# Two lone mixers of a diffusion transformer: four delta-net chunks prepared together, then four state steps

## The chip, the cores and the metric

One core of a Trainium2 chip. The metric is the device time of one execution in microseconds.

## What is computed

Two layers of a transformer block over 256 latent tokens (s = 0) and 256 context tokens (s = 1), width 1024. Each layer modulates by columns computed from a condition (`silu(c) @ ada_w`), runs a hybrid mixer (attention beside a gated delta rule in both directions) and then a PEER feed-forward, which fetches 128 experts per token from tables.

```python
mod_lat = (jax.nn.silu(c) @ ada_w[l] + ada_b[l])[:, None, :]
h_lat = rmsnorm(x, norm1_w[l]) * (1.0 + sc1) + sh1
...
A = jnp.where(strict, jnp.einsum('nbhid,nbhjd->nbhij', kb, kc) * decay, 0.0)
Tm = jnp.eye(C, dtype=jnp.float32) + A
u = lax.linalg.triangular_solve(Tm, vc * bc[..., None], ...)
w = lax.linalg.triangular_solve(Tm, kb * jnp.exp(gcum)[..., None], ...)
qk = jnp.einsum('nbhid,nbhjd->nbhij', qc, kc) * decay
def step(S, xs):
    v_new = u_i - jnp.einsum('bhcd,bhde->bhce', w_i, S)
    o_i = (jnp.einsum('bhcd,bhde->bhce', q_i * jnp.exp(g_i)[..., None], S)
           + jnp.einsum('bhij,bhje->bhie', qk_i, v_new))
    S = (S * jnp.exp(g_last)[..., None]
         + jnp.einsum('bhcd,bhce->bhde', k_i * jnp.exp(g_last - g_i)[..., None], v_new))
...
x = x + g1 * o_lat
x = x + g2 * peer_ffn(h2, peer_wq[l], peer_subkeys[l], peer_u[l], peer_v[l])
```

The inverse of `Tm`, `w` and `qk` of a chunk need no state S; only `step` does.

## The kernel before

Of the four mixers two run with nothing beside them: mixer(1, 0) at the start and mixer(0, 1) in the middle. They are called with `big=True` and write each operand of their projections as a high and a low part (`_hi`, `_lo`; `whi`, `wlo` for weights), three matmuls for one. The other two mixers lie under the fetching of experts.

A lone mixer runs in this order. `norm1` (L345) squares and scales the two token tiles (128 tokens each; `xn`), transposes them into the bank `ps_n`, and applies scale and shift on ScalarE (`hf`), from which `hT_hi` and `hT_lo` are made. `dn_gates` makes the gates g and beta from `ps_ba`; `dn_project` makes q, k and v (`ps_dn`), one weight tile of 512 KB for 128 columns. Then `dn_scan` (L733) runs over 2 x 2 chunks: token tiles 0 and 1 forward (d = 0), 1 and 0 backward (d = 1). `dn_chunk` (L605) is the state-free part: gate sums (`ps_g`), decay (`ps_R`, E), `ps_KK`, the mask B, the start of X and its transpose M, `ps_QK`, and six levels that build the inverse; a level is `ps_P` from M and B, its copy Pm on ScalarE, `ps_X` from X and Pm, and VectorE's masked copy into X (`COPY_PREDICATED X<-clev,ps_X`) with M transposed anew. `dn_step` (L698) is the step with the state: `ps_y`, `ps_o`, `ps_S`. Before, the two chunks of a step i go through `dn_chunk` in lockstep, their two `dn_step` follow, and then comes the next pair.

Beside the scan runs a filler, one of its pieces per yield times `rate`: attention's projections (`ps_pr` from `in_rows`), attention itself (`ps_as`, `ps_pT`, `ps_ao`), the gate's projection, and then `modulation` (L279) of chunks 4 to 9. What of the filler is left when the scan ends follows it, and then chunk 10. These seven chunks read 28 weight tiles `ada_t`, for each two matmuls into `ps_ada`, after four of them a copy `row` and four small matmuls into `ps_adat`. These lines decide the order of the filler and of the splits:

```python
for _ in main:            # _with_filler
    due += n
    while due >= 1:
        next(filler, None)
        due -= 1
...
w = (pool or self.wpool).tile([P, D], F32, tag="w", name="w")     # weight, L194
self.nc.sync.dma_start(w, self.ap[name][l, i])
...
hi = self.hlpool.tile([P, D], F32R, tag="whi", name="whi")
lo = self.hlpool.tile([P, D], F32R, tag="wlo", name="wlo")
self.split(w, hi, lo)
```

wpool has four buffers; a weight's load is issued on SyncE's queue once the matmuls of the tile four before it are done. hlpool holds the split parts; the split is a cast on ScalarE (whi) and a subtraction on VectorE (wlo). After the scan `dn_output` norms O (`dO`) and multiplies it by the gate, transposes it (`ps_yT`), and the out projection reads `out_t`.

A scheduler sets the final order of each engine's instructions from the code's order and its own estimate of times, so the order below is read from the built program. All VectorE work is recorded under L131, the line of a helper.

Of the kernel before, what the change touches and what calls it, by code (L numbers as in the profile page):

```python
# [20 lines left out]
P = 128  # L21
# [125 lines left out]
class Net:  # L147
# [196 lines left out]
    def norm1(self, pool, s, pr, hl):  # L344
# [3 lines left out]
        with self.pool(f"n1{s}") as pn:  # L348
            ss = pn.tile([P, 2 * NT], F32, name="n1ss")
            xn = []  # L350
            for t in range(NT):
                for n in range(2):
                    self.square_sum(pn, x, ss, t, n)
# [3 lines left out]
                xn.append(xt)  # L357
            for g in range(KB // 2):
                ps = self.dbank("ps_n1")
                for j in range(2):  # L360
                    for t in range(NT):
                        self.transpose(ps[:, j * T + t * P : j * T + t * P + P], xn[t][:, _blk(2 * g + j, P)])
                for j in range(2):
                    kb = 2 * g + j
                    a, b = pr["acol"][:, s, 0, kb : kb + 1], pr["mod"][:, s, kb : kb + 1]
                    if hl:
                        f = pn.tile([P, T], F32, tag="hf", name="hf", bufs=2)
                        hi, lo = (part[:, kb, :] for part in h)
# [3 lines left out]
                    elif j == 0:  # L372
                        self.dve.tensor_scalar(h[0][:, kb, :], ps[:, _blk(j, T)], a, b, op0=ALU.mult, op1=ALU.add)
                    else:
                        nc.scalar.activation(h[0][:, kb, :], ps[:, _blk(j, T)], AF.Identity, bias=b, scale=a)
# [227 lines left out]
    def dn_chunk(self, pool, dn, t, d, it):  # L603
# [11 lines left out]
        def mk(name):  # L615
            return pool.tile(shape, F32, tag=f"{name}{d}", name=f"{name}{d}")
# [83 lines left out]
    def dn_step(self, pool, it, vtok, d, S, O, first_o, new_S):  # L700
# [7 lines left out]
        y = pool.tile([P, DNH, P], F32, tag=f"Pm{d}", name="y")  # L708
# [24 lines left out]
    def dn_scan(self, pool, dn, s, O):  # L733
# [43 lines left out]
    def mixer(self, s, l, pr, big, filler=(), rate=1, late_mods=(), late_consts=None):  # L777
# [4 lines left out]
        with self.pool("mx" + nm) as pa:  # L782
# [533 lines left out]
```

## Time and profile before

| | us |
|---|---|
| runs of the kernel | 2882.13, 2885.86, 2894.39 (median 2885.86) |
| profiled execution | 2888.39, span 2886.6 |
| first lone mixer: first scan | 111 to 259 |
| second lone mixer: second scan | 1961 to 2126 |

TensorE is busy for 65% of the span, VectorE for 64%, ScalarE for 37%, GpSimd for 32%, and the mean granted clock of TensorE is 0.735 of full speed. These are means over stages of very different kinds: while experts are fetched, the DMA engines are busy at 0.9 and more; in the lone mixers hardly any expert moves, and each engine's own table counts. So the lone mixers have to be read in their own stretches.

### The profile page before, as it was taken

What the parts mean: (1) busy time and instruction counts of PE and PEld (TensorE: products, weight loads), DVE (VectorE), ACT (ScalarE), POOL (GpSimd) and SP (SyncE); (2) the same over time, 40 slices, a digit from 0 to 9 for tenths busy, and PEclk for the clock granted to TensorE, in tenths of its full rate; (3) what the DMA queues carried; (4) which work ended last, traced back from release to release, by engine and by line L of the source; (5) the groups of instructions that cost most, each with busy time, mean ns of one, the idle gap of its engine ahead of it and who ended that gap; (6) DMA issues with size and microseconds to landing.
All of it is one profiled execution on the core that took longest, in us unless ns stands there. A gap on an engine that the chain in (4) does not pass through costs nothing.

```text
span 2886.6 us, 37977 instructions
## 1 busy us (share of the span) xinstructions
PE 1888.9 (65%) x12928; PEld 1089.0 (38%) x12928; DVE 1837.9 (64%) x4902; ACT 1066.9 (37%) x2583; POOL 918.4 (32%) x772
## 2 busy tenths in 40 slices
PE   7998844478768888445876644488989544434444
PEld 5876721044336556111544400077767210000000
DVE  4854598465477768974676644487545986544444
ACT  4532333265354334332644322264233332222222
POOL 0000234433244432443243444200002444435552
PEclk8999965579889999556888855599999655555555
DMA  7334799999989999999999999831258999999997
GB/s 281 106 110 168 261 359 363 419 418 364 333 314 364 390 378 390 378 419 418 382 384 371 418 420 419 343 122 40 106 187 302 419 419 419 419 370 420 419 420 293
DMA packets 163311, 961.60 MB, mean 333 GB/s; under 512 B 20784, under 2 KB 28336, under 8 KB 64816
## 3 DMA queue, kind: packets, MB, share of 16 engines
q0 software_dynamic: 110592, 805.36, 69.2%
q1 hardware_dynamic: 52528, 153.83, 15.3%
q8 instruction: 104, 1.70, 0.2%
q14 instruction: 87, 0.71, 0.1%
HBM read 945.48 MB, written 1.05 MB: 328 GB/s over the span
## 4 chain that ended last, share of the span: by engine, by line
DMA 40%; PE 30%; DVE 18%; ACT 6%; issue 4%; POOL 1%; SPq 0%; POOLq 0%; DVEq 0%; ACTq 0%
DMA G<-in_peer_uv,idx 35%; DVE junk L131 6%; PE ps_pq L899 4%; PE acc L1084 3%; DMA h2r<-h 2%; PE ps_P L675 2%; PE ps_dn L208 2%; PE ps_pr L208 2%; PE ps_X L681 2%; PE ps_ada L298 1%; PE ps_pr L211 1%; PE ps_pr L210 1%; PE ps_pr L212 1%; DVE si L131 1%; DMA w<-in_ada_t 1%
## 5 line engine op out<-in xcount | busy, mean ns | idle before, releaser
L1039 POOL DMA_INDIRECT G<-in_peer_uv,idx x768 | 918.2, 1196 | 1934.3 <-PE acc L1084 743.3
L131 DVE CUSTOM_DVE_ANT_0 junk<-G,h2r 128x1024 bf16<-128x1024 f32 x768 | 937.3, 1220 | 511.0 <-DMA G<-in_peer_uv,idx 496.7
L1084 PE MATMUL acc<-G,dg 128*32 128x256 f32 x6144 | 704.9, 550 | 826.5 <-ACT dg L1080 823.2
L1084 PEld LDWEIGHTS acc<-G,dg 128*32 128x32 f32 x6144 | 148.7, 129 | 1321.2 <-ACT dg L1080 1275.8
L1079 ACT ACTIVATE dg<-cident,act 128x32 f32<-128x32 f32 x768 | 246.6, 321 | 1067.4 <-DVE act L131 1031.4
L1080 ACT ACTIVATE dg<-dg,pgate 128x32 f32<-128x32 f32 x768 | 246.4, 321 | 23.3
L899 PE MATMUL ps_pq<-h2T,w 128*128 128x256 f32 x768 | 181.0, 396 | 0.0
L899 PEld LDWEIGHTS ps_pq<-h2T,w 128*128 128x128 f32 x768 | 151.0, 200 | 28.2 <-issue 7.4
L675 PE MATMUL ps_P<-M,B 128*128 128x128 f32 x768 | 115.5, 299 | 32.4 <-DVE M L131 29.5
L675 PEld LDWEIGHTS ps_P<-M,B 128*128 128x128 f32 x768 | 101.5, 206 | 66.4 <-issue 30.7
L131 DVE COPY_PREDICATED X<-clev,ps_X 128x512 f32<-128x512 int8 x96 | 69.7, 728 | 72.6 <-PE ps_X L681 72.6
L681 PE MATMUL ps_X<-X,Pm 128*128 128x128 f32 x768 | 106.1, 284 | 2.4 <-ACT Pm L677 2.4
L681 PEld LDWEIGHTS ps_X<-X,Pm 128*128 128x128 f32 x768 | 95.9, 196 | 18.2 <-issue 7.5
L131 DVE TENSOR_TENSOR wlo<-w,whi 128x1024 fp32r<-128x1024 f32 (+1 forms) x66 | 78.7, 1194 | 36.7 <-ACT whi L181 36.7
L677 ACT COPY Pm<-ps_P 128x512 f32<-128x512 f32 x96 | 56.0, 584 | 121.4 <-PE ps_P L675 121.2
L181 ACT CAST whi<-w 128x1024 fp32r<-128x1024 f32 (+1 forms) x66 | 67.3, 1023 | 71.6 <-PE ps_pr L212 36.3
L1079 ACT ACT_TABLE_LOAD x60 | 77.0, 1283 | 22.1 <-DVE act L131 21.2
L208 PE MATMUL ps_dn<-hT,w 128*128 128x256 f32 x320 | 84.0, 423 | 0.0
L298 PE MATMUL ps_ada<-w,silc 128*32 128x512 f32 x384 | 75.5, 640 | 10.7 <-DMA w<-in_ada_t 10.7
L131 DVE SCALAR_TENSOR_TENSOR cy<-craw,cw,cy 128x256 f32<-128x256 f32 x176 | 81.1, 482 | 1.6
L208 PEld LDWEIGHTS ps_dn<-hT,w 128*128 128x128 f32 x320 | 67.0, 215 | 16.9 <-issue 6.5
L131 DVE MAX8 sv<-sc 128x8 f32<-128x128 f32 x192 | 47.5, 283 | 39.6 <-ACT sc L911 38.7
(294 smaller groups left out, 2757.3 us busy)
## 6 DMA issues: line engine op xcount, KB each, us to landing
w<-in_ada_t SPq DMA_DIRECT2D x96, 512.0 KB, 6.3
w<-in_wq_t SPq DMA_DIRECT2D x48, 512.0 KB, 8.5
w<-in_in_dn SPq DMA_DIRECT2D x44, 512.0 KB, 8.7
w<-in_in_rows SPq DMA_DIRECT2D x40, 512.0 KB, 4.3
w<-in_out_t SPq DMA_DIRECT2D x24, 512.0 KB, 5.1
h2r<-h SPq DMA_DIRECT2D x96, 128.0 KB, 10.0
G<-in_peer_uv,idx POOLq DMA_INDIRECT x768, 16.4
skT<-in_skT SPq DMA_DIRECT2D x24, 128.0 KB, 5.2
```

The lines of the kernel that those rows point to most:

```text
L131: ins = op(*args, **kw)
L181: self.nc.scalar.copy(hi, x)
L208: self.nc.tensor.matmul(out, lhs[0], rhs[0], start=first, stop=last)
L298: nc.tensor.matmul(ps[_blk(g, 32), :], self.silc[:, kb, :], w[:, _blk(k, CW)], start=(kb < 4), stop=(kb >= 4))
L675: nc.tensor.matmul(pp[:, _blk(h, P)], B[:, h, :], M[:, h, :], start=True, stop=True)
L677: nc.scalar.copy(_flat(Pm), pp)
L681: nc.tensor.matmul(xp[:, _blk(h, P)], Pm[:, h, :], X[:, h, :], start=True, stop=True)
L899: nc.tensor.matmul(ps[:, _blk(j, T)], w[:, _blk(kb, P)], hT[:, kb, :], start=(kb == 0), stop=(kb == KB - 1))
L1039: self.nc.gpsimd.indirect_dma_start(out=G, out_offset=None, in_=self.ap[f"peer_uv{l}"], in_offset=bass.IndirectOffsetOnAxis(ap=idx, axis=0))
L1079: nc.scalar.activation(dg, self.ident4, AF.Gelu, scale=a)
L1080: nc.scalar.mul(dg, dg, un["gate"][:, m, j : j + 1])
L1084: nc.tensor.matmul(self.acc[_blk((j + q) % QUADS, QP), _blk(q, QD)], dg, G[:, D + QD * q : D + QD * q + QD], start=(un["first"] and m == 0 ...
```

## The change

Five edits. `dn_scan` takes `together`; in the lone mixers the state-free parts of all four chunks run in lockstep first, each with tiles of its own (a key for direction and step), and the four state steps follow. The filler's rate goes from 1.85 to 3.3. hlpool has two buffers where it had three, in both lone mixers. The pool "ma" with the normed input opens before the mixer's other pools, so that it lies lowest in SBUF, and stays open to the mixer's end. And `norm1` goes token tile by token tile: squares, scale, transposes of four blocks into a bank, four 128x128 ScalarE ops, one split of 4x128; in the mixers that aren't big, 16 ops of 128 columns stand for 8 of 256.

```diff
@@ norm1
             for t in range(NT):
+                ss = pn.tile([P, 2 * NT], F32, name=f"n1ss{t}")
                 for n in range(2):
                     self.square_sum(pn, x, ss, t, n)
                 rs = self.rms_scale(pn, ss[:, t::NT], 1, f"n1{t}")
                 xt = pn.tile([P, D], F32, name=f"xn{t}")
                 self.dve.tensor_scalar_mul(xt, x[t], rs)
-                xn.append(xt)
-            for g in range(KB // 2):
-                ps = self.dbank("ps_n1")
...
-                        nc.scalar.activation(f, ps[:, _blk(j, T)], AF.Identity, bias=b, scale=a)
+                for g in range(2):
+                    ps = self.dbank("ps_n1")
+                    for j in range(4):
+                        self.transpose(ps[:, _blk(j, P)], xt[:, _blk(4 * g + j, P)])
+                    f = None
+                    if hl:
+                        f = pn.tile([P, 4, P], F32, tag="hf", name="hf", bufs=2)
+                    for j in range(4):
+                        kb = 4 * g + j
...
+                        if hl or j % 2:
+                            nc.scalar.activation(to, ps[:, _blk(j, P)], AF.Identity, bias=b, scale=a)
+                        else:
+                            self.dve.tensor_scalar(to, ps[:, _blk(j, P)], a, b, op0=ALU.mult, op1=ALU.add)
@@ dn_chunk
-            return pool.tile(shape, F32, tag=f"{name}{d}", name=f"{name}{d}")
+            return pool.tile(shape, F32, tag=name + it["key"], name=f"{name}{d}")
@@ dn_scan
-        for i in range(NT):
-            its = [{}, {}]
-            ts = (i, NT - 1 - i)
-            yield from _zip(*[self.dn_chunk(pool, dn, ts[d], d, its[d]) for d in range(2)])
+        its = [[{"key": f"{d}{i}" if together else f"{d}"} for d in range(2)] for i in range(NT)]
+        order = [(i, NT - 1 - i) for i in range(NT)]
+
+        def chunks(*steps):
+            return _zip(*[self.dn_chunk(pool, dn, order[i][d], d, its[i][d]) for i in steps for d in range(2)])
+
+        if together:
+            yield from chunks(*range(NT))
+        for i, ts in enumerate(order):
+            if not together:
+                yield from chunks(i)
             for d in range(2):
@@ mixer
-        with self.pool("mx" + nm) as pa:
+        with ExitStack() as outer:
+
+            h = self.norm1(outer.enter_context(self.pool("ma" + nm)), s, pr, hl) if big else None
+            pa = outer.enter_context(self.pool("mx" + nm))
...
-                        _with_filler(self.dn_scan(pd, dn, s, O), rows(pc), rate)
+                        _with_filler(self.dn_scan(pd, dn, s, O, True), rows(pc), rate)
@@ both calls of a lone mixer
-                    self.hlpool = pool("hl0", 3, st)
+                    self.hlpool = pool("hl0", 2, st)
...
-                        1, 0, prs[0], True, mods(0, range(4, 10), 1), 1.85,
+                        1, 0, prs[0], True, mods(0, range(4, 10), 1), 3.3,
```

Where the instructions stand is seen at three places. First TensorE in the first lone mixer, where the ada matmuls begin. Before, it is behind attention's last `ps_ao` and in the first of the second pair's levels:

```order
L493 MATMUL ps_ao<-apT,av 128x256 x2
L298 MATMUL ps_ada<-w,silc 32x512 x8
L675 MATMUL ps_P<-M_1861,B_1856 128x128 x4
L675 MATMUL ps_P<-M_1873,B_1868 128x128 x4
L306 MATMUL ps_adat<-quads,row 128x2 x4
L298 MATMUL ps_ada<-w,silc 32x512 x2
L681 MATMUL ps_X<-X_1858,Pm_1919 128x128 x4
L681 MATMUL ps_X<-X_1870,Pm_1926 128x128 x4
L298 MATMUL ps_ada<-w,silc 32x512 x6
L675 MATMUL ps_P<-M_1861,B_1856 128x128 x4
L306 MATMUL ps_adat<-quads,row 128x2 x4
L675 MATMUL ps_P<-M_1873,B_1868 128x128 x4
```

In the changed program the levels of all four chunks, the `ps_w` and two state steps stand ahead of the first ada matmul. Between the last two steps four more tiles (two matmuls each) are mixed in, and the end of the stage, up to the first `ps_yT`, reads:

```order
L718 MATMUL ps_S<-y,B_2097 128x128
L298 MATMUL ps_ada<-w,silc 32x512 x2
L306 MATMUL ps_adat<-quads,row 128x2 x4
L298 MATMUL ps_ada<-w,silc 32x512 x8
L306 MATMUL ps_adat<-quads,row 128x2 x4
L298 MATMUL ps_ada<-w,silc 32x512 x8
L306 MATMUL ps_adat<-quads,row 128x2 x4
L298 MATMUL ps_ada<-w,silc 32x512 x8
L306 MATMUL ps_adat<-quads,row 128x2 x4
L298 MATMUL ps_ada<-w,silc 32x512 x8
L306 MATMUL ps_adat<-quads,row 128x2 x4
L163 MATMUL ps_yT<-ident,dO 128x128 x8
```

The ada matmuls have moved from the second pair's levels to behind attention, and their last four rounds of four tiles stand alone on TensorE.

Second, ScalarE at the norm of the second lone mixer, where the experts' last results (`G<-acc`, `G<-turn`) are copied. `res_x_79` and `res_x_80` are token tiles 0 and 1. Before:

```order
L1093 COPY G<-acc 128x512 x2
L1106 COPY G<-turn 128x512 x2
L336 ACTIVATE sq,n1ss<-res_x_79 128x512
L657 COPY X_13748<-ident 128x512
L657 COPY X_13760<-ident 128x512
L336 ACTIVATE sq,n1ss<-res_x_79 128x512
L336 ACTIVATE sq,n1ss<-res_x_80 128x512 x2
L369 ACTIVATE hf<-ps_n_12901,mod,acol 128x256 x2
L369 ACTIVATE hf<-ps_n_12914,mod,acol 128x256 x2
L369 ACTIVATE hf<-ps_n_12927,mod,acol 128x256 x2
L369 ACTIVATE hf<-ps_n_12940,mod,acol 128x256 x2
L552 ACT_TABLE_LOAD
```

In the changed program:

```order
L1106 COPY G<-acc 128x512 x2
L1119 COPY G<-turn 128x512
L336 ACTIVATE sq,n1ss_12905<-res_x_80 128x512
L1119 COPY G<-turn 128x512
L368 ACTIVATE hf<-ps_n_12881,mod,acol 128x128 x4
L336 ACTIVATE sq,n1ss_12905<-res_x_80 128x512
L551 ACT_TABLE_LOAD
L551 ACTIVATE ea<-alog 128x8
L656 COPY X_13852<-ident 128x512
L368 ACTIVATE hf<-ps_n_12893,mod,acol 128x128 x4
```

Tile 0's squares are no longer in this piece; they stand earlier, among the experts' ops, and tile 0's hf stands between the two squares of tile 1.

Third, VectorE in the first lone mixer, between the norm and the gates, where weights are split (`wlo<-w,whi`, a tile of 128x1024 each) and the level masks are cast (`clev`). Before:

```order
L131 CAST hT_hi<-hf 128x256
L131 TENSOR_TENSOR hT_lo<-hf,hT_hi 128x256
L131 CAST hT_hi<-hf 128x256
L131 TENSOR_TENSOR hT_lo<-hf,hT_hi 128x256
L131 MEMSET craw 128x2 x6
L131 TENSOR_TENSOR wlo<-w,whi 128x1024
L131 COPY ba<-ps_baT 128x32
L131 CAST clev<-clevf 128x1792
L131 TENSOR_SCALAR beta<-ba 128x16
L131 TENSOR_TENSOR z<-ba,dtb 128x16
```

In the changed program:

```order
L131 CAST hT_hi<-hf 128x4x128
L131 TENSOR_TENSOR hT_lo<-hf,hT_hi 128x4x128
L131 CAST hT_hi<-hf 128x4x128
L131 TENSOR_TENSOR hT_lo<-hf,hT_hi 128x4x128
L131 CAST clev<-clevf 128x1792
L131 TENSOR_TENSOR wlo<-w,whi 128x1024
L131 COPY ba<-ps_baT 128x32
L131 TENSOR_SCALAR beta<-ba 128x16
L131 TENSOR_TENSOR z<-ba,dtb 128x16
```

The split that stood ahead of `ba` and of the cast of clev stands behind the cast; of three splits of whole tiles ahead of the cast, one is left. SyncE's queue issues the same loads in the same order in both lone mixers.

## Rows read from the trace of the kernel before

**Rows 1.** Chain that ended last, whole span: shares by engine and line.

```profile
DMA G<-in_peer_uv,idx 35%; DVE junk L131 6%; PE ps_pq L899 4%; PE acc L1084 3%; DMA h2r<-h 2%; PE ps_P L675 2%; PE ps_dn L208 2%; PE ps_pr L208 2%; PE ps_X L681 2%; PE ps_ada L298 1%; PE ps_pr L211 1%; PE ps_pr L210 1%; PE ps_pr L212 1%; DVE si L131 1%; DMA w<-in_ada_t 1%
```

**Rows 2.** Stretches: length; busy (x count) by engine; PEclk; DMA share; GB/s.

```profile
111.00:259.00 148.00, 130.62 (x935) 105.70 (x933) 88.96 (x219) 53.49 (x101) 0.00 (x0) 0.97 0.33 115
...
111.00:133.00 22.00, 22.00 (x123) 19.84 (x122) 19.40 (x57) 11.82 (x21) 0.00 (x0) 0.87 0.07 26
...
242.80:254.00 11.20, 9.66 (x82) 9.08 (x81) 3.23 (x8) 1.99 (x4) 0.00 (x0) 1.00 0.29 95
...
1961.00:2126.00 165.00, 145.49 (x999) 120.32 (x997) 98.77 (x227) 54.39 (x99) 0.00 (x0) 0.92 0.29 103
...
2120.00:2130.00 10.00, 4.30 (x18) 3.91 (x19) 7.13 (x23) 3.74 (x7) 0.00 (x0) 0.52 0.50 179
```

**Rows 3.** Instruction groups by form, 111 to 258 us: busy, mean ns | idle before.

```profile
L298 PE MATMUL ps_ada<-w,silc 128*32 128x512 f32 x112 | 20.7, 603 | 0.5 <-DMA w<-in_ada_t 0.5
...
L306 PE MATMUL ps_adat<-quads,row 128*128 128x2 f32 x56 | 6.7, 241 | 0.0
...
L653 PE MATMUL ps_KK<-dkT 128*128 128x128 f32 x32 | 5.1, 326 | 0.0
...
L665 PE MATMUL ps_QK<-dqT,dkT 128*128 128x128 f32 x32 | 4.1, 279 | 0.0
...
L163 PE MATMUL ps_R<-ident,gc 128*128 128x128 f32 x16 | 3.0, 349 | 0.0
...
L131 DVE SCALAR_TENSOR_TENSOR E<-ps_R,gc,cmats 128x128 f32<-128x128 f32 x16 | 4.5, 343 | 0.0
...
L131 DVE TENSOR_TENSOR qkt<-ps_QK,E 128x512 f32<-128x512 f32 x4 | 2.7, 681 | 0.0
```

**Rows 4.** Ada loads: issues; landing from 187 and from 223 us; DMA from 10 us.

```profile
187.79 41.95 SPq L197 DMA_DIRECT2D w<-in_ada_t  x24
...
DMA to landing us min/median/max: 6.4/6.7/7.1
...
DMA to landing us min/median/max: 4.4/4.4/4.4
...
DMA packets 1137, 4.13 MB, mean 413 GB/s; under 512 B 128, under 2 KB 128, under 8 KB 1137
```

**Rows 5.** Timeline of TensorE, first scan: start, us, line, tile.

```profile
111.08 0.42 PE L625 MATMUL ps_g<-g,cmats 128*128 128x4 f32 x2
...
186.69 1.50 PE L298 MATMUL ps_ada<-w,silc 128*32 128x512 f32 x12
...
258.92 1.52 PE L163 MATMUL ps_yT<-ident,dO 128*128 128x128 f32 x5 [5.01 <-DVE dO L131]
```

**Rows 6.** Timeline of VectorE, first scan.

```profile
133.46 0.73 DVE L131 COPY_PREDICATED X<-clev,ps_X 128x512 f32<-128x512 int8 x1
```

**Rows 7.** Timeline of TensorE, second scan.

```profile
1960.82 0.42 PE L625 MATMUL ps_g<-g,cmats 128*128 128x4 f32 x2
...
2065.28 1.92 PE L298 MATMUL ps_ada<-w,silc 128*32 128x512 f32 x16
...
2125.70 1.50 PE L163 MATMUL ps_yT<-ident,dO 128*128 128x128 f32 x5 [6.59 <-DVE dO L131]
```

**Rows 8.** Timeline of ScalarE, norm of the second lone mixer.

```profile
1880.11 1.14 ACT L657 COPY X<-ident 128x512 f32<-128x512 f32 x2 [0.90 <-ACT sq L336]
...
1881.90 0.63 ACT L336 ACTIVATE sq<-res_x 128x512 f32<-128x512 f32 x1
...
1888.02 1.02 ACT L369 ACTIVATE hf<-ps_n,mod,acol 128x256 f32<-128x256 f32 x2 [4.64 <-PE ps_n L163]
...
1892.42 1.21 ACT L369 ACTIVATE hf<-ps_n,mod,acol 128x256 f32<-128x256 f32 x2 [0.26 <-DVE hT_lo L131]
```

**Rows 9.** Timeline of VectorE, first lone mixer's projections.

```profile
44.89 1.23 DVE L131 TENSOR_TENSOR wlo<-w,whi 128x1024 fp32r<-128x1024 f32 x1 [1.54 <-ACT whi L181]
...
49.16 1.09 DVE L131 CAST clev<-clevf 128x1792 int8<-128x1792 f32 x1 [2.94 <-DMA clevf<-in_k_levels]
```

More of the change, by code (lines that the diff above doesn't have):

```diff
@@ L356, in norm1 @@
                 self.dve.tensor_scalar_mul(xt, x[t], rs)
-                xn.append(xt)
-            for g in range(KB // 2):
-                ps = self.dbank("ps_n1")
[L360 to L365, printed above, removed]
-                    if hl:
-                        f = pn.tile([P, T], F32, tag="hf", name="hf", bufs=2)
-                        hi, lo = (part[:, kb, :] for part in h)
-                        nc.scalar.activation(f, ps[:, _blk(j, T)], AF.Identity, bias=b, scale=a)
+                for g in range(2):
[3 more added lines that the diff above has]
+                    f = None
+                    if hl:
+                        f = pn.tile([P, 4, P], F32, tag="hf", name="hf", bufs=2)
+                    for j in range(4):
+                        kb = 4 * g + j
+                        a, b = pr["acol"][:, s, 0, kb : kb + 1], pr["mod"][:, s, kb : kb + 1]
+                        to = f[:, j, :] if hl else h[0][:, kb, _blk(t, P)]
+                        if hl or j % 2:
[3 more added lines that the diff above has]
+                    if hl:
+                        hi, lo = (part[:, 4 * g : 4 * g + 4, _blk(t, P)] for part in h)
                         self.dve.tensor_copy(hi, f)
                         self.dve.tensor_tensor(lo, f, hi, op=ALU.subtract)
[L372 to L375, printed above, removed]
         return h
@@ L626, in dn_chunk @@
         nc.tensor.matmul(gp[:, 4:8], self.ones, g, start=True, stop=True)
-        gc = pool.tile([P, 8], F32, tag=f"gc{d}", name="gc")
+        gc = pool.tile([P, 8], F32, tag="gc" + it["key"], name="gc")
         v.tensor_copy(gc, gp[:, 0:8])
-        ex = pool.tile([P, 12], F32, tag=f"ex{d}", name="ex")
+        ex = pool.tile([P, 12], F32, tag="ex" + it["key"], name="ex")
         v.tensor_tensor(ex[:, 8:12], gc[:, 4:8], gc[:, 0:4], op=ALU.subtract)
@@ L707, in dn_step @@
                 nc.tensor.matmul(yp[:, _blk(h, P)], it["nwT"][:, h, :], S[:, h, :], start=False, stop=True)
-        y = pool.tile([P, DNH, P], F32, tag=f"Pm{d}", name="y")
+        y = pool.tile([P, DNH, P], F32, tag="Pm" + it["key"], name="y")
         nc.scalar.copy(_flat(y), yp)
@@ L748, in dn_scan @@
                 o = None if O is None else O[:, ts[d]]
-                self.dn_step(pool, its[d], dn["vtok"][:, ts[d]], d, st[d], o, ts[d] not in seen, new_S)
+                self.dn_step(pool, its[i][d], dn["vtok"][:, ts[d]], d, st[d], o, ts[d] not in seen, new_S)
                 seen.add(ts[d])
@@ L795, in mixer @@
             dn = dict(g=g, beta=beta, ktok=ktok, vtok=vtok, kT=kT, qT=qT)
-            with self.pool("ma" + nm) as pb:
-                h = self.norm1(pb, s, pr, hl)
+            with ExitStack() as inner:
+                if not big:
+                    h = self.norm1(inner.enter_context(self.pool("ma" + nm)), s, pr, hl)
                 first = 0 if full else 4
@@ L1202, in build @@
                     psums(st, 4, 4)
[L1203 removed]
+                    self.hlpool = pool("hl2", 2, st)
                     self.mixer(
[L1205 removed]
+                        0, 1, prs[1], True, mods(1, range(4, 10), 1), 3.3,
                         [mods(1, (c,)) for c in (10, 11)],
```

8 lines of the change are left out of this document (2 added, 6 removed).

## The prediction

> **What bounds the kernel now.** I read the chain that ended last first: 35% of it is the expert gathers, in the four stretches in which experts are fetched [rows 1]. The change does not touch those stretches. So it can act only where the gathers stop and a lone mixer runs by itself: from the start to about 290 us, and from 1870 to about 2170 us. A microsecond won or lost there shows in the end time one for one, since each lone mixer's result is what the next gathers are computed from.
>
> The table of stretches comes next [rows 2]. In the first scan (111 to 259 us) TensorE is busy for 130.62 of 148 us, in the second (1961 to 2126) for 145.49 of 165. TensorE is therefore nearly the bound: about 17 and 20 us are idle, and no reordering inside a scan can win more than that and what a slow clock costs (mean granted clock 0.97 and 0.92 of full speed). Then the groups of instructions of the first scan: the ada matmuls cost 20.7 us, and TensorE waits only 0.5 us for their weights [rows 3], because 24 tiles of 512 KB arrive, issued over 41.95 us [rows 4], under the levels of the second pair of chunks. That cover is what the change takes away.
>
> **Where the marks stand.** In the first scan the first gate sum (ps_g) is at 111.08, the first ada matmul at 186.69, the first transpose of the normed output (ps_yT) at 258.92, after 5.01 us idle on VectorE's dO [rows 5]. VectorE's first in-level update of X is at 133.46 [rows 6], 22.4 us behind ps_g. In the second scan the marks are 1960.82, 2065.28 and 2125.70, the last after 6.59 us idle [rows 7]. I forecast each mark in turn, with T0 for the first ada matmul.
>
> **Norm by tiles, second mixer.** On ScalarE the copies into X and tile 0's second square take from 1880.11 to 1881.90, before tile 1's squares, and hf of both tiles takes from 1888.02 to 1893.63 [rows 8]. In ScalarE's new order tile 0's squares and its first four hf stand ahead of tile 1's second square, and all but one of the copies into X behind hf: 1.8 us of the first stretch and half of the second, 2.8, go from the way. That is -4.6; I take -4.5 us, between 0 (tile 0's work waits behind the experts' last ops) and -6.
>
> **Early weights, first mixer.** Before, VectorE splits two more weight tiles ahead of the cast of clev, which waits until 49.16 for its DMA; the third ends at 46.1 [rows 9]. With two split buffers only one stands ahead of that cast, so the last of these three splits, done at 46.1 before, comes behind the cast's end at 50.25 and ends near 51.5, 5.4 us later. Part of that was lead over TensorE, which is still at the tile ahead. I take +3 (0 to +5.4), so ps_g at 114.1. In the second mixer the cast isn't there; +1 with the -4.5 puts ps_g at 1957.3.
>
> **The state-free head.** All four chunks now go through decay, KK, QK and mask before the first level's update of X. VectorE was busy 19.40 of 22 us there for two chunks [rows 2]. Each more chunk adds its share of the E ops, 4.5 / 4 = 1.1 us, and seven 128x512 ops like qkt at 2.7 / 4 = 0.68 [rows 3]: 5.9 us, or 5.8 without the overlap of their ends. Two gate ops of that size moved in, 1.2. So 22.4 + 2 x 5.8 + 1.2 = 35.2, and I add 2.5 for the first copies and transposes until TensorE is fed at full rate: 37.7 us. TensorE has the 22.0 us that it did before and two chunks' KK, QK and R, half of 5.1 + 4.1 + 3.0 = 6.1 [rows 3]: 28.1. A hole of 9.6 us opens.
>
> **Levels and steps up to T0.** The work of TensorE in the scan stays. Of 130.62 us in the first scan, ada takes 20.7 and adat 6.7 [rows 3], and two steps 9.66 [rows 2]; these come behind T0 now. With 28.1 in the head, 65.5 us are left between the head and T0. Four chunks in lockstep leave TensorE something to do while VectorE and ScalarE turn one chunk around, so I add 2 us of waits only (0 to 8). T0 = 114.1 + 37.7 + 65.5 + 2 = 219.3 (before 186.69). In the second scan 145.49 - 37.1 - 28.1 = 80.3 us are left, and T0 = 1957.3 + 37.7 + 80.3 + 2 = 2077.3 (before 2065.28).
>
> **The ada stream.** The order of DMAs is the same: four tiles are there, and 24 follow as slots come free, now with only the last two steps beside them. In the trace the first loads are issued 1.1 us after the first ada matmul and, four in flight, land in 6.4 to 7.1 us; two in flight land in 4.4 [rows 4]. A slot's cycle is its landing and about 1.1 us of use and reissue. No stretch here shows this stream undisturbed, so I bound it: (4.4 + 1.1) / 4 = 1.38 us a tile below, (6.7 + 1.1) / 4 = 1.95 above, near the 41.95 / 23 = 1.82 at which the loads were issued under the levels. I take 1.55: with deeper prefetch the same tiles come at 413 GB/s [rows 4], 1.27 us each, four of them in 5.1 us, and (5.1 + 1.1) / 4 = 1.55. From T0 to yT: 7.5 to the first new tile, 23 x 1.55 = 35.7, 2 for its matmuls and adat: 45.2 us. TensorE has 37.1 us of work in it, so the stream sets the end, and VectorE's norm of the output, for which yT waited 5 to 6.6 us, is hidden: the last step comes four rounds of tiles before the end.
>
> yT is then at 264.5 (before 258.92: **+5.6**) and 2122.5 (before 2125.70: **-3.2**). The out projection's first weights are issued later than before, as ada's slots empty, and have two split buffers: +1 in each mixer (0 to +4). SBUF placement, tile keys and the 128-wide norm ops of the other mixers lie under the gathers and cost nothing; were that cover gone, eight ops more at no more than half of hf's 1.02 for a pair [rows 8] are at most 4 us.
>
> **Sum.** +5.6 - 3.2 + 2 = +4.4 us, on the profiled execution's 2888.39: 2892.8. The median of the runs shown is 2.5 lower, so I forecast 2890 for it. This is no change that can be measured: the runs before spread over 12 us, and I call anything within 0.5% (14.4 us) the same.
>
> **A rule against the change.** Before both yT TensorE stood idle, and the clock granted just after was below full speed: 0.52 of it, which is 1.2 GHz, in 2120 to 2130 us [rows 2]. The ada stream now has such waits between its batches. The Trainium skill, TensorE: Matmul & The Clock Gate, section "HAM oscillation — how this bites in real kernels", says that a loop whose batch of matmuls is shorter than the wait for its next weights falls back to the slow clock in each turn. The trace agrees for single waits; no stretch of it shows the loop. What it would cost here is the second slower rival.
>
> **Rivals.**
> *Faster.* The hole is smaller and the stream quicker: gate rows and attention fill the head down to a hole of 4 us (-5.6 each), the levels run without a wait (-2), the stream takes 1.38 a tile (-4). That is -11.6 in each scan, and 4.4 - 23.2 = -18.8 against the kernel before: 2867. For it: the idle before both yT goes, and of the second scan's 20 us of idle and its clock of 0.92 lockstep should spare a part. Against: VectorE was busy 19.4 of 22 us in the head already. It decides from a T0 of about 211 and 2069. Chance 0.26.
> *Slower, by the stream.* Four slots without work beside them keep to 1.95 a tile: 23 x 0.4 = +9.2 in each scan, 2890 + 18.4 = 2908. For it: landings of 6.4 to 7.1 with four in flight. Against: 4.4 where fewer were. From 1.77 a tile it is slower than before beyond what can be told. Chance 0.15.
> *Slower, by the clock.* Each batch of four tiles starts at half speed: a tile's use, 20.7 / 28 = 0.74 us by the row, doubles, so 0.74 / 4 = 0.18 a tile or +4.3 a scan, and the out projection starts slow, some +2 each: +12.6, 2903. For it: the row at 2120. Against: the waits are short pieces between tiles that land one by one. Chance 0.09.
> *No change.* The terms as above, one scan later, one earlier. Chance 0.50.
>
> **Range.** The slow end is the first slower rival, the fast end the faster one; what is left out is the case in which several terms go the same way. 2868 to 2908; the likeliest case alone 2876 to 2900. Faster by over 0.5%: 0.26; within: 0.50; slower: 0.24.
>
> **What the trace after would show.** ps_g near 114 and 1957; the first in-level update of X 35 us later, with TensorE idle for some 10 us in between; first ada near 219 and 2077; between it and yT a DMA share above 0.8 with TensorE waiting for w, 45 us long; no idle on dO before yT; hf's end near 1889. I am wrong if T0 comes 8 us earlier (the head was not VectorE's), if TensorE hardly waits for w in the stream, or if splits (wlo) hold the projections back: then the two buffers cost more than +1.

## The result, and the profile after

The changed kernel takes 2901.34 us (median of 9 runs, 2894.58 to 2911.95) against 2887.30 us of the kernel before (9 runs, 2882.13 to 2894.39): a ratio of 1.0051, 95% interval 1.0037 to 1.0065. It is about 14 us slower, at the edge of what was called the same, and inside the forecast range; the forecast of 2890 was 11 us too low. The profiled execution took 2909.75 us (span 2908.0), 8 us above its median (the kernel before's, at 2888.39, is 1 above its own), so a stretch of it may be some us long by chance.

The marks of both scans on TensorE's timeline, to be read beside [rows 5] and [rows 7]:

```profile
112.72 0.28 PE L624 MATMUL ps_g<-g,cmats 128*128 128x4 f32 x2
...
212.62 1.92 PE L298 MATMUL ps_ada<-w,silc 128*32 128x512 f32 x16
...
263.84 1.95 PE L163 MATMUL ps_yT<-ident,dO 128*128 128x128 f32 x8
...
1977.46 0.28 PE L624 MATMUL ps_g<-g,cmats 128*128 128x4 f32 x2
...
2095.65 1.92 PE L298 MATMUL ps_ada<-w,silc 128*32 128x512 f32 x16
...
2141.72 0.74 PE L163 MATMUL ps_yT<-ident,dO 128*128 128x128 f32 x5
```

From ps_g to ps_yT the first scan takes 151.1 us (147.8 before), the second 164.3 (164.9). Both yT now follow other work: the idle on dO is gone. Inside, the balance is another one. T0 comes 99.9 and 118.2 us behind ps_g (75.6 and 104.5 before), and from T0 to yT it is 51.2 and 46.1 us. Stretches of the first scan as in [rows 2]; the first is the whole scan, the second the head up to VectorE's first in-level update of X, the third the stretch from T0 to yT, the fourth a part of that:

```profile
113.00:264.00 151.00, 133.37 (x932) 104.58 (x932) 86.87 (x224) 52.33 (x101) 0.00 (x0) 0.96 0.30 107
113.00:150.00 37.00, 31.35 (x207) 28.41 (x207) 34.09 (x93) 19.04 (x34) 0.00 (x0) 0.95 0.13 44
213.00:264.00 51.00, 43.07 (x247) 20.36 (x240) 11.14 (x41) 8.15 (x14) 0.00 (x0) 0.92 0.78 283
240.00:260.00 20.00, 15.30 (x68) 4.60 (x68) 0.76 (x5) 1.73 (x3) 0.00 (x0) 0.83 0.85 302
```

In the head VectorE is busy 34.09 of 37 us, TensorE 31.35. It ends with VectorE's first in-level update of X, on VectorE's timeline (beside [rows 6]):

```profile
149.54 1.95 DVE L131 COPY_PREDICATED X<-clev,ps_X 128x512 f32<-128x512 int8 x3
```

From T0 to yT the DMA engines are busy at 0.78 and TensorE stands idle for 8 of 51 us. The groups of the whole scan, as in [rows 3]:

```profile
L298 PE MATMUL ps_ada<-w,silc 128*32 128x512 f32 x112 | 26.7, 696 | 4.2 <-DMA w<-in_ada_t 4.2
L306 PE MATMUL ps_adat<-quads,row 128*128 128x2 f32 x56 | 7.8, 262 | 3.7 <-ACT row L303 3.7
```

Busy time of ada has gone from 20.7 to 26.7 us for the same 112 matmuls, and the waits ahead of ada and adat from 0.5 and 0 to 4.2 and 3.7: with nothing beside it, each copy of `row` on ScalarE stands open on TensorE too.

The span can be cut at marks that all kernels have: the first ps_pq (the first lone mixer is over), the first ps_ba of the second lone mixer (the gathers are over), and its first ps_pq. Between the two profiled executions the first piece grew by 7.1 us, the gathers by 11.1, the second lone mixer by 2.6, the rest by 0.6. That is 21.4 us where the medians differ by 14.0, so some 7 us of it are these two executions' own; but about half of the growth lies where I had put nothing.

### The profile page after: what moved, and what is told of

It is laid out like the page before. It is cut to its first block, busy times and chain, and to the rows that moved or that the text cites. A ratio compares the mean times of both kernels' runs of the same rounds, so it can differ in the third digit from the quotient of the medians.

```text
span 2908.0 us, 37989 instructions
## 1 busy us (share of the span) xinstructions
PE 1900.1 (65%) x12928; PEld 1082.1 (37%) x12928; DVE 1833.8 (63%) x4894; ACT 1068.3 (37%) x2607; POOL 918.9 (32%) x772
## 3 DMA queue, kind: packets, MB, share of 16 engines
HBM read 945.48 MB, written 1.05 MB: 325 GB/s over the span
## 5 line engine op out<-in xcount | busy, mean ns | idle before, releaser
L1097 PE MATMUL acc<-G,dg 128*32 128x256 f32 x6144 | 713.5, 556 | 820.3 <-ACT dg L1093 803.1
L131 DVE CUSTOM_DVE_ANT_0 junk<-G,h2r 128x1024 bf16<-128x1024 f32 x768 | 936.6, 1220 | 494.5 <-DMA G<-in_peer_uv,idx 475.9
L131 DVE TENSOR_TENSOR wlo<-w,whi 128x1024 fp32r<-128x1024 f32 (+1 forms) x66 | 78.7, 1193 | 56.2 <-ACT whi L181 55.7
L298 PE MATMUL ps_ada<-w,silc 128*32 128x512 f32 x384 | 90.3, 703 | 20.1 <-DMA w<-in_ada_t 20.0
L680 PE MATMUL ps_X<-X,Pm 128*128 128x128 f32 x768 | 99.6, 277 | 0.1
L131 DVE COPY_PREDICATED X<-clev,ps_X 128x512 f32<-128x512 int8 x96 | 68.5, 723 | 45.3 <-PE ps_X L680 45.0
L131 DVE SCALAR_TENSOR_TENSOR cy<-craw,cw,cy 128x256 f32<-128x256 f32 x176 | 80.9, 480 | 1.7
L131 DVE MAX8 sv<-sc 128x8 f32<-128x128 f32 x192 | 47.5, 283 | 42.0 <-ACT sc L924 38.8
L208 PEld LDWEIGHTS ps_dn<-hT,w 128*128 128x128 f32 x320 | 67.2, 215 | 16.5 <-issue 6.1
```

The source lines that it names most:

```text
L131: ins = op(*args, **kw)
L208: self.nc.tensor.matmul(out, lhs[0], rhs[0], start=first, stop=last)
L298: nc.tensor.matmul(ps[_blk(g, 32), :], self.silc[:, kb, :], w[:, _blk(k, CW)], start=(kb < 4), stop=(kb >= 4))
L680: nc.tensor.matmul(xp[:, _blk(h, P)], Pm[:, h, :], X[:, h, :], start=True, stop=True)
L1097: nc.tensor.matmul(self.acc[_blk((j + q) % QUADS, QP), _blk(q, QD)], dg, G[:, D + QD * q : D + QD * q + QD], start=(un["first"] and m == 0 ...
```

## The experiments

Each was run in five rounds beside the kernel before, on the same chip as it. The kernel before had medians of 2887.43, 2884.89 and 2888.04 us in the three sittings of the experiments, so close kernels of different sittings are to be compared by their ratios. The table has the pieces just named from each one's profiled execution, as differences of start times on TensorE's timeline, and the two columns at the end concern mixer (0, 0) under the gathers: how the 12 loads of in_rows (plain numbers) and 16 copies of h2r (numbers with an h) follow each other in SyncE's queue, and the time from its first ps_g to its first ps_as.

| kernel | ratio to before (95%) | to first ps_pq | gathers | second mixer | queue of mixer (0, 0) | ps_g to ps_as |
|---|---|---|---|---|---|---|
| before | 1 | 300.6 | 1589.0 | 277.3 | 10, 4h, 1, 4h, 1, 8h | 59.6 |
| changed | 1.0051 (1.0037 to 1.0065) | 307.6 | 1600.1 | 279.9 | 9, 8h, 2, 8h, 1 | 66.5 |
| zip | 0.9958 (0.9944 to 0.9973) | 291.6 | 1599.3 | 264.8 | 9, 8h, 2, 8h, 1 | 66.6 |
| quarter | 0.9944 (0.9927 to 0.9960) | 291.5 | 1599.3 | 262.4 | 9, 8h, 1, 4h, 1, 4h, 1 | 64.5 |
| hl2 | 0.9992 (0.9980 to 1.0004) | 305.9 | 1577.2 | 280.9 | 9, 4h, 2, 4h, 1, 8h | 56.4 |
| newnorm | 1.0033 (1.0021 to 1.0045) | 299.4 | 1596.7 | 275.9 | 9, 8h, 2, 8h, 1 | 65.9 |
| oldnorm | 0.9984 (0.9971 to 0.9998) | 303.8 | 1575.3 | 280.5 | 11, 8h, 1, 8h | 54.2 |
| phase | 0.9992 (0.9980 to 1.0004) | 304.1 | 1580.7 | 275.1 | 11, 8h, 1, 8h | 56.6 |
| lone | 1.0014 (1.0005 to 1.0023) | 309.9 | 1583.9 | 278.9 | 10, 4h, 1, 4h, 1, 8h | 54.7 |
| actq | 1.0064 (1.0051 to 1.0078) | 304.1 | 1601.1 | 278.9 | 12, no h | 57.3 |
| pace | 1.0009 (1.0000 to 1.0019) | 300.9 | 1592.2 | 278.8 | 9, 4h, 1, 4h, 1, 8h, 1 | 64.1 |
| zip_oldnorm | 0.9931 (0.9917 to 0.9945) | 291.5 | 1588.0 | 265.9 | 10, 4h, 1, 4h, 1, 8h | 60.9 |
| zip_phase | 0.9910 (0.9898 to 0.9923) | 292.1 | 1582.5 | 266.5 | 11, 8h, 1, 8h | 54.9 |
| zip_old_p4 | 0.9915 (0.9902 to 0.9928) | 292.2 | 1586.1 | 265.1 | 11, 8h, 1, 8h | 52.0 |

**zip: the ada chunks beside attention.**

```diff
-                        yield from _zip(att, self.proj_rows((h,), "in_rows", l, 2, use_gate, hl))
+                        yield from _zip(att, self.proj_rows((h,), "in_rows", l, 2, use_gate, hl), filler if big else iter(()))
```

> The changed kernel with one edit: the six chunks of ada weights run beside attention and the gate's projection instead of behind them, so that their 24 loads arrive while the levels of the four chunks run. Theory (the stream of ada weights behind attention sets the end of each scan): each scan ends 6 to 12 us earlier than in the changed kernel, the out projection's first weights are there in time (1 to 3 us each), and the whole is 14 to 28 us faster than the changed kernel, so 0.99 to 1.00 of the kernel before. Rival (the split buffers or the norm hold the time): within 5 us of the changed kernel, 1.003 to 1.007 of the kernel before.

Measured 2874.29 us, the upper end of what the theory gave. From ps_g to ps_yT the scans take 134.6 and 152.4 us, 16.5 and 11.9 less than in the changed kernel, the first more than expected. Its first scan as a stretch, with the columns of [rows 2]:

```profile
113.00:248.00 135.00, 126.05 (x934) 101.13 (x933) 89.03 (x222) 52.96 (x101) 0.00 (x0) 0.99 0.36 129
```

And its ada group there, as in [rows 3]:

```profile
L298 PE MATMUL ps_ada<-w,silc 128*32 128x512 f32 x112 | 21.2, 601 | 0.0
```

The same 112 ada matmuls are back at 21.2 us and wait for nothing; TensorE is busy 126.05 of 135 us. From ps_yT to ps_pq, the out projection's stretch, only the second mixer got time back (42.7 us, 45.9 in the changed kernel; in the first 44.2 and 43.8), so that part of the expectation came in half.

**quarter: a quarter of the loads, all of the matmuls.**

```diff
-                (w,) = self.weight("ada_t", l, 4 * n + q, False, self.first_weights)
+                if q == 0 or not 4 <= n <= 10:
+                    (w,) = self.weight("ada_t", l, 4 * n + q, False, self.first_weights)
```

> The changed kernel with one ada weight tile loaded for each of chunks 4 to 10 of a layer and used for all four quarters, so that 7 of 28 loads of a scan are left and the matmuls all stay; this leaves out three quarters of that weight matrix. Theory (the loads set the end of the scan behind attention): from the first ada matmul to ps_yT 34 to 40 us instead of 46 to 51, 15 to 25 us in all, 0.996 to 1.000 of the kernel before. Rival (TensorE's matmuls, the copies of rows and adat set it): within 6 us of the changed kernel, 1.003 to 1.005.

Measured 2871.46 us. T0 and yT in the first scan:

```profile
213.84 1.92 PE L299 MATMUL ps_ada<-w,silc 128*32 128x512 f32 x16
...
247.78 1.52 PE L163 MATMUL ps_yT<-ident,dO 128*128 128x128 f32 x6
```

34 us for 51, with T0 where it was (101.6 us behind ps_g, 99.9 in the changed kernel): the loads set the end of the changed kernel's scan. The gain, 30 us, is larger than 15 to 25. From ps_g to yT the two scans are 15.6 and 13.6 us shorter, which is nearly all of it, and the second mixer's out projection starts sooner too (ps_yT to ps_pq is 41.5 us, 45.9 in the changed kernel; in the first mixer it gained nothing).

**hl2: two split buffers in the kernel before.**

```diff
-                    self.hlpool = pool("hl0", 3, st)
+                    self.hlpool = pool("hl0", 2, st)
```

(and the same for hl2)

> The kernel before with two split buffers for three in both lone mixers, nothing else. Theory (the buffers are a small term): +1 to +4 us, 1.000 to 1.0015 of the kernel before. Rival (the two buffers make most of the loss): +9 us or more, 1.003 to 1.007, with TensorE idle for wlo in the projections.

The whole is no slower, 2883.30 us, and that hides two effects of opposite sign: the lone mixers are 5.3 and 3.6 us longer, the gathers 11.8 shorter. The projections ahead of the first scan lose nothing (ps_g at 110.86, 111.08 before). Of the first mixer's 5.3 us, 4.1 lie between ps_g and yT, where attention's projections run as filler, and 1.4 behind; of the second's 3.6, 2.8 lie behind yT. TensorE's waits for wlo, in the first scan and in the out projection:

```profile
126.54 0.50 PE L211 MATMUL ps_pr<-wlo,hT_hi 128*128 128x512 f32 x1 [2.50 <-DVE wlo L131]
...
272.94 0.50 PE L211 MATMUL ps_pr<-wlo,mixD_hi 128*128 128x512 f32 x1 [0.53 <-DVE wlo L131]
```

These waits are 3 of the 5.3 us; what makes the rest isn't shown. That the gathers moved though no buffer of theirs was changed was the first sign that the order of the mixers under the gathers is touched by edits elsewhere.

**newnorm and oldnorm: the norm alone, and all but the norm.** norm1 of the change put into the kernel before (newnorm), and norm1 of before put into the changed kernel (oldnorm). The edit of newnorm, cut to its core (oldnorm is the same with the signs exchanged):

```diff
-            for g in range(KB // 2):
-                ps = self.dbank("ps_n1")
-                for j in range(2):
-                    for t in range(NT):
-                        self.transpose(ps[:, j * T + t * P : j * T + t * P + P], xn[t][:, _blk(2 * g + j, P)])
...
+                for g in range(2):
+                    ps = self.dbank("ps_n1")
+                    for j in range(4):
+                        self.transpose(ps[:, _blk(j, P)], xt[:, _blk(4 * g + j, P)])
...
```

> The kernel before with the norm by token tiles in all four mixers, nothing else. Theory (the earlier end of hf is given back, since ba's matmuls wait for the second tile of every block): -2 to +2 us, 0.999 to 1.001. Rival A (it helps by the 4.5 us that were forecast): 0.998 to 0.999. Rival B (the 128-wide ops of the other two mixers slow the stretch of the gathers): +3 to +6 us, 1.001 to 1.002.

> The changed kernel with the norm of before in all four mixers; the rest of the change stays. Theory: within 3 us of the changed kernel, 1.003 to 1.007 of the kernel before, so the loss is not the norm's. Rival B (the norm costs under the gathers): 4 us or more faster than the changed kernel, 1.000 to 1.003.

My theory failed in both: newnorm is 10 us slower than before, oldnorm 19 us faster than the changed kernel. Both go rival B's way, and further than it said. In the lone mixers the norm is worth little either way (newnorm -1.1 and -1.4 us); the difference lies under the gathers: 1597 to 1600 us in the changed kernel, zip, quarter and newnorm, which have the new norm, and 1575 to 1589 in oldnorm, hl2 and the kernel before, which have the old one.

**phase: all of the new norm, but the pace put back.** VectorE's work in the mixers under the gathers drives a pace counter (`Paced`, L131): each op adds 0.1 + size / 960, and at 1.0 (or 0.7) a piece of the experts' work is put in. Eight ops of 128 columns for four of 256 make 0.4 more, so that all later pieces stand elsewhere.

```diff
+        if not hl:
+            self.dve.due -= 0.4
         return h
```

> The changed kernel with a bookkeeping edit alone: after the norm of the two mixers that lie under the gathers, the pace counter is put back by 0.4, the amount by which their 16 ops of 128 columns count more than 8 of 256. Every op of the norm stays. In SyncE's queue of mixer (0, 0) the last in_rows weight then stands behind 8 copies of h2r, not 16. Theory (the loss under the gathers is that weight's place in the queue): the stretch from the first mixer's end to the second's start 1575 to 1590 us instead of 1600, the whole 8 to 20 us faster than the changed kernel, 0.998 to 1.002 of the kernel before. Rival (the 128-wide ops themselves): like the changed kernel, 1.003 to 1.007.

2884.28 us, 17 us less than the changed kernel with each op of the norm in place. The rival, that the 128-wide ops themselves cost it, is out. SyncE's queue in mixer (0, 0) of the changed kernel (start, time over the whole group, line, copy):

```profile
724.81 6.43 SPq L948 DMA_DIRECT2D h2r<-h  x8
731.34 1.70 SPq L197 DMA_DIRECT2D w<-in_in_rows  x2
736.12 11.04 SPq L948 DMA_DIRECT2D h2r<-h  x8
748.46 0.33 SPq L197 DMA_DIRECT2D w<-in_in_rows  x1
```

and, in the kernel of phase, the same place of SyncE's queue:

```profile
720.30 7.19 SPq L950 DMA_DIRECT2D h2r<-h  x8
727.59 0.53 SPq L197 DMA_DIRECT2D w<-in_in_rows  x1
728.21 15.54 SPq L950 DMA_DIRECT2D h2r<-h  x8
```

The last weight of attention's and the gate's projections is issued at 748.46 behind all 16 copies of h2r, and at 727.59 behind 8 of them with the pace put back. TensorE's timeline where it waits for those weights, the last groups of ps_pr, in the changed kernel:

```profile
746.68 3.70 PE L208 MATMUL ps_pr<-w,hT 128*128 128x512 f32 x8 [1.62 <-DMA w<-in_in_rows]
...
759.84 5.87 PE L208 MATMUL ps_pr<-w,hT 128*128 128x512 f32 x8 [7.87 <-DMA w<-in_in_rows]
```

and in phase, the one group there that waits for a weight:

```profile
743.27 3.70 PE L208 MATMUL ps_pr<-w,hT 128*128 128x512 f32 x8 [3.10 <-DMA w<-in_in_rows]
```

A wait of 7.87 us against 3.10; and the last weight is issued 31.8 us behind the mixer's first ps_g against 15.6, 16 us later.

**lone: the new norm in the lone mixers only.** The others call norm1_wide, which is norm1 of before under another name.

```diff
-                    h = self.norm1(inner.enter_context(self.pool("ma" + nm)), s, pr, hl)
+                    h = self.norm1_wide(inner.enter_context(self.pool("ma" + nm)), s, pr, hl)
```

> The changed kernel with the norm of before in the two mixers that lie under the gathers; the lone mixers keep the norm by tiles. The last in_rows weight of mixer (0, 0) stands behind 8 copies of h2r. Both theories expect the stretch under the gathers at 1575 to 1590 us and 0.998 to 1.002 of the kernel before; a third one, that the norm in the lone mixers makes the loss, expects 1.003 to 1.007.

2889.53 us: 12 us less than the changed kernel, as both expected; the norm in the lone mixers isn't the main loss. Some of it may be: against oldnorm, from which it differs by that norm alone, lone is 7 us longer, with intervals that don't touch (1.0005 to 1.0023, 0.9971 to 0.9998). Between the two profiles 8.7 us lie under the gathers and 4.5 in the lone mixers, and lone's is 5 us above its median, so where these 7 us come from stays open.

**actq: h2r from ScalarE's queue.**

```diff
-                self.nc.sync.dma_start(t[_blk(b, QP), :], h2[_blk(j, QP), :])
+                self.nc.scalar.dma_start(t[_blk(b, QP), :], h2[_blk(j, QP), :])
```

> The changed kernel with the copies of h2r issued from ScalarE's queue, so that no in_rows weight stands behind them. Theory (the weight's place in SyncE's queue): TensorE's wait of 8 us for the last in_rows weight of mixer (0, 0) goes, the stretch under the gathers takes 1570 to 1590 us, 0.997 to 1.002 of the kernel before, less whatever ScalarE loses by 16 issues a block. Rival (the 128-wide ops): the wait goes but the stretch stays near 1600, 1.003 to 1.007.

2906.08 us, so the queue theory's sum fails and the rival's figures come true: the wait goes, the gathers take 1601 us, the ratio is 1.0064. The rival's cause, the 128-wide ops, is out by phase all the same. The place that the edit was made for did what the queue theory said: ps_g to ps_as takes 57.3 us, 9.1 less. But the copies now stand in ScalarE's own order. Sixteen of them on ScalarE's queue, and its waits from 1140 to 1600 us (engine, line and what it waited for: us in total, times, longest):

```profile
1140.73 20.36 ACTq L948 DMA_DIRECT2D h2r<-h  x16
...
ACT sc L924 <- DMA h2r<-h: 22.1, 1, 22.1
...
ACT dg L1092 <- DMA h2r<-h: 14.2, 1, 14.2
```

Behind mixer (0, 0) it was given back: from its first ps_pq to the first ps_ba of mixer (1, 1) it is 332.8 us (324.7 in the changed kernel), and from there to the second lone mixer's first ps_ba 522.1 (518.4). That ScalarE's waits make this is likely, since they lie in these two stretches, but no run tests it. What I had set aside in a half sentence ("less whatever ScalarE loses") would then have decided it.

**pace: the kernel before with the counter put forward.** The same edit with the other sign, at the end of the old norm1.

```diff
+        if not hl:
+            self.dve.due -= -0.4
         return h
```

> The kernel before with one bookkeeping edit: after the norm of the two mixers under the gathers the pace counter is put forward by 0.4, as the narrower norm ops of the change put it. No op is added or changed. In SyncE's queue of mixer (0, 0) the last in_rows weight then stands behind 16 copies of h2r, not 8. Theory (the place in the queue): the stretch from ps_g to ps_as of mixer (0, 0) takes 64 to 67 us instead of 60, and the whole 1.002 to 1.005 of the kernel before. Rival (what the norm's own ops cost): 0.999 to 1.001.

The local part came true (64.1 us from ps_g to ps_as), the whole did not: 1.0009, within the rival's range. The stretch ahead of it, first ps_ba to first ps_g of mixer (0, 0), gave 6.8 us back (115.6 for 122.3). So a weight's place in the queue costs its wait, but not each wait reaches the end.

**zip_oldnorm, zip_phase, zip_old_p4: both gains together.** The edit of zip with the norm of before, with the pace put back by 0.4, and with both (the norm of before has the lower pace by itself; zip_old_p4 goes 0.4 further). The edits of zip_phase; the other two have norm1 of before besides:

```diff
+        if not hl:
+            self.dve.due -= 0.4
         return h
...
-                        yield from _zip(att, self.proj_rows((h,), "in_rows", l, 2, use_gate, hl))
+                        yield from _zip(att, self.proj_rows((h,), "in_rows", l, 2, use_gate, hl), filler if big else iter(()))
```

(zip_oldnorm has the second edit only.)

> The changed kernel with the ada chunks beside attention and the norm of before in all mixers. If the two gains add: 18 us from the stream of ada weights and 10 to 20 from the stretch under the gathers, 2855 to 2870 us, 0.988 to 0.994 of the kernel before, faster than both kernels and than the one with the ada chunks alone moved. If the stretch under the gathers only differed by chance: 0.995 to 0.997, as that one.

> The changed kernel with the ada chunks beside attention and the pace counter put back by 0.4, the norm by tiles kept. Lone mixers as in the kernel with the chunks alone moved (some 21 us less than before), the stretch under the gathers 1575 to 1585 us: 2852 to 2862 us, 0.988 to 0.992. If the stretch under the gathers stays at 1588 or above, the place of the last in_rows weight is not all of it: 0.993 or above.

> As the last one, but with the norm of before in all mixers and the pace counter put back by 0.4 behind it. The last in_rows weight stands behind 8 copies of h2r, and the one before it behind none, as there: 2852 to 2864 us, 0.988 to 0.992. If the norm by tiles is worth something in the lone mixers by itself, this one is 2 to 6 us slower than the last.

2866.93, 2864.06 and 2862.60 us. zip_phase is 2 us above the range given for it, the others are inside theirs. Most of the two gains adds up: zip alone was 27 us below the changed kernel and phase 17, zip_phase is 37 below it. All three beat both kernels. zip_oldnorm and zip_phase count to the same pace and are 2.9 us apart with intervals that overlap, but they differ in the queue's order as well as in the norm. zip_phase and zip_old_p4 have the same order in mixer (0, 0) and differ in the norm, and can't be told apart: no gain of the norm by tiles is shown.

## Why the forecast held, and which terms were off

The forecast said: no change that can be measured, +4.4 us, one scan later, one earlier. The scans did that nearly as worked out, in part by luck, since errors in them cancelled; their mechanism, ada weights arriving with nothing beside them, is shown by zip and quarter. The first lone mixer as a whole grew by 7.1 us (forecast +6.6), the second, from the last residual on, by 3.1 (forecast -2.2), and the rest lies under the gathers. The terms, forecast and measured between the profiled executions:

| term | forecast | measured |
|---|---|---|
| first mixer up to ps_g | +3 | +1.6 |
| first scan, ps_g to yT | +2.6 | +3.3 |
| second mixer from the last residual to ps_g | -3.5 | about -1 |
| second scan | +0.3 | -0.6 |
| yT to ps_pq, both | +2 | +6.9 |
| under the gathers | 0 | +11.1 (in all 21.4 here, 14.0 by the medians) |

**Head and stream.** Two errors cancelled. The head is VectorE's, as said: the first in-level update of X comes 36.8 us behind ps_g (forecast 35.2). But TensorE found more to do in it (31.35 of 37 us, a hole of 5.7 and not 9.6), and T0 was 99.9 us behind ps_g, not 105.2. The stream was 51.2 us, not 45.2. Its first new tile came 4.8 us behind T0, not 7.5; from there (217.37) to its last (260.48) it took 43.1 / 23 = 1.87 us a tile, near the upper bound of 1.95 and not at 1.55.

```profile
217.37 1.05 PE L298 MATMUL ps_ada<-w,silc 128*32 128x512 f32 x4 [0.28 <-DMA w<-in_ada_t]
...
260.48 1.05 PE L298 MATMUL ps_ada<-w,silc 128*32 128x512 f32 x4 [1.35 <-DMA w<-in_ada_t]
```

In the second scan the sums were 118.2 (forecast 120.0) and 46.1 (45.2). That the scans' sums came so near to the forecast is luck; that the loads set their end is not, as quarter shows. The filler's rate and the place of the pool "ma" weren't run by themselves.

**The clock.** The slower rival by the clock came in part. In 240 to 260 us the mean granted clock was 0.83: a part of that stretch ran at 1.2 GHz. The Trainium skill, TensorE: Matmul & The Clock Gate, "HAM oscillation — how this bites in real kernels", describes a loop whose batches are shorter than the waits for their weights and all start slow. Here a tile's matmuls took 1.05 us and the waits for w, where there were any, 0.2 to 1.5; and most of the stream ran at 2.4 GHz (0.92 in 213 to 264), so not every batch started slow. What the slow part cost wasn't measured by itself.

**The norm by tiles.** The step that failed is "1.8 us of the first stretch and half of the second, 2.8, go from the way". The half of the second stretch did go, the 1.8 us went and came back: hf ends 11.0 us after the end of the last residual add, where it was 13.6. That add and the first and last step of tile 1's scale (`tot`, `xn`), on VectorE's timeline of the kernel before:

```profile
1879.34 0.69 DVE L131 TENSOR_TENSOR res_x<-res_x,G 128x512 f32<-128x512 f32 x1
...
1883.41 0.16 DVE L131 TENSOR_TENSOR tot<-n1ss 128x1 f32<-128x1 f32 x1 [0.39 <-ACT sq L336]
...
1886.28 0.75 DVE L131 TENSOR_SCALAR xn<-res_x,n_y 128x1024 f32<-128x1024 f32 x1
```

the same of the changed kernel:

```profile
1896.97 0.69 DVE L131 TENSOR_TENSOR res_x<-res_x,G 128x512 f32<-128x512 f32 x1
...
1898.63 0.16 DVE L131 TENSOR_TENSOR tot<-n1ss 128x1 f32<-128x1 f32 x1 [0.18 <-ACT sq L336]
...
1902.06 0.43 DVE L131 CAST hT_hi<-hf 128x512 fp32r<-128x512 f32 x1 [1.45 <-ACT hf L368]
...
1903.71 0.75 DVE L131 TENSOR_SCALAR xn<-res_x,n_y 128x1024 f32<-128x1024 f32 x1
```

and on ScalarE's, the first and the last hf, between them a table load (ACT_TABLE_LOAD):

```profile
1896.48 1.50 ACT L368 ACTIVATE hf<-ps_n,mod,acol 128x128 f32<-128x128 f32 x4 [0.27 <-PE ps_n L163]
...
1898.62 1.28 ACT L551 ACT_TABLE_LOAD   x1
...
1905.73 2.90 ACT L368 ACTIVATE hf<-ps_n,mod,acol 128x128 f32<-128x128 f32 x8 [2.15 <-issue]
```

Counted from the add's end, tile 1's squares are summed 2.4 us sooner, but xn starts only 0.2 us sooner (at 6.05 us, 6.25 before): tile 0's splits now stand among the small ops of tile 1's scale, and one of them waits 1.45 us for an hf that stands behind the table load.

And I followed hf and not its reader. A ba matmul reads a block of both tiles. Before, two blocks came whole at a time, and ba's matmuls ran beside the next ones; the last was over 1.3 us after hf. Now the second tile's half of each block comes last, no ba matmul can start ahead of 1907.75, and all 24 run one after the other behind it (TensorE's timeline, the first and the last):

```profile
1907.75 0.39 PE L210 MATMUL ps_ba<-hT_hi,whi 128*16 128x256 f32 x1 [1.25 <-DVE hT_hi L131]
...
1912.23 0.28 PE L212 MATMUL ps_ba<-hT_hi,wlo 128*16 128x256 f32 x1
```

What 2.6 us were won ahead, ba took back: its last matmul ends 14.9 us behind the add's end in both kernels.

**Two split buffers.** Forecast +3 and +1 in the projections and +1 for each out projection. The +3 for early weights is not borne out: hl2, which has the two buffers alone, reaches ps_g 0.2 us sooner than the kernel before, and the changed kernel's +1.6 is no more than newnorm (+1.4) and pace (+1.2) show with three buffers. The loss comes later, +5.3 and +3.6 in hl2's two mixers, with TensorE held by wlo in the first scan and in the out projection, as the prediction's own sign of being wrong says ("then the two buffers cost more than +1"). For the out projection "+1 in each mixer" was too small: 2.1 and 4.7 us in the changed kernel, of which hl2 has 1.4 and 2.8.

**Under the gathers.** The step that failed outright is "SBUF placement, tile keys and the 128-wide norm ops of the other mixers lie under the gathers and cost nothing", with its bound of 4 us and, ahead of it, "The change does not touch those stretches". The ops do cost next to nothing (phase keeps them all). What they move is the pace counter, and with it the order in which the experts' work and its DMAs stand among the mixer's; 17 us hang on that in the changed kernel. In 13 profiles the time from ps_g to ps_as in mixer (0, 0) is 64.1 to 66.6 us where the last in_rows weight stands behind 16 copies of h2r, 52.0 to 60.9 where it stands behind 8. The gathers as a whole take 1592 to 1600 us in the former and 1575 to 1589 in the latter.

How the local wait becomes the whole's can be read from the DMA engines. The stretch from ps_g to ps_as in mixer (0, 0), before, changed and in phase, with the columns of [rows 2] (the fifth engine is GpSimd):

```profile
713.03:772.65 59.62, 44.18 (x218) 18.03 (x217) 29.80 (x63) 20.91 (x46) 16.56 (x14) 0.83 0.95 303
...
716.64:783.12 66.48, 50.43 (x222) 21.00 (x221) 29.34 (x62) 20.39 (x44) 14.04 (x13) 0.78 0.83 271
...
711.96:768.54 56.58, 41.83 (x223) 17.30 (x221) 29.97 (x63) 21.23 (x46) 14.46 (x14) 0.86 1.01 334
```

and from the same mixer's first ps_pq to the first ps_ba of mixer (1, 1), before and changed:

```profile
1053.96:1369.93 315.97, 190.72 (x1345) 98.75 (x1345) 230.65 (x847) 109.97 (x308) 119.03 (x102) 0.69 1.00 400
...
1064.69:1389.39 324.70, 196.60 (x1355) 99.77 (x1354) 232.62 (x853) 111.15 (x315) 118.79 (x103) 0.68 0.99 394
```

In the first stretch, in which TensorE waits for the weight, the DMA engines of the changed kernel stand idle for 0.17 of 66.48 us, some 11 us, against 3 before and none in phase. The largest growth, 8.7 us, then lies in the second, where they are busy all the time and have 1.3 MB more to move. Summed over the gathers from the packets of each trace, the DMA engines are busy for 1510 to 1522 us in all 14 kernels and idle for 71 us before, 85 in the changed kernel, 62 in phase, 78 in newnorm and 73 in pace. So what a wait costs the whole is the DMA time that stays lost: 14 us more than before in the changed kernel, 2 in pace, though the stretch from ps_g to ps_as is nearly as long there (64.1 us for 66.5). Why pace makes it good elsewhere no run shows, and all this is read from one profile a kernel.

## What to carry to other kernels

Weights that come through few buffers belong beside the longest stretch of other matmuls, not behind it: the same 28 tiles cost 28 us more in two scans when a filler reached them last. Where a pace, a counter or a scheduler sets the order, compare every queue over the whole program, SyncE's too: an edit of 0.4 in a counter was worth more than the edit that it came with. And to tell an op's cost from that of the order that it makes, undo the bookkeeping and keep the op.

## What the runs showed of the hardware that was not expected

Four buffers of 512 KB brought 283 GB/s with TensorE waiting for them, where the prefetch of 15 tiles at the start had 413 [rows 4]: in a closed loop of four slots the DMA engines were busy for 0.78 of the time, while TensorE waited for loads. And sixteen copies issued from ScalarE's queue took 20.4 us of its order in one place, so that the next op there, which reads none of them, began after 22.1 us of idle (actq).
